# Six pairs of channel tiles in a 4096-to-2048 float32 projection: seven block products of sums for eight block products

## The chip, the cores and the metric

The kernel runs on one core of a Trainium2 chip. The metric is device time in microseconds (us) of that core, as the median of several executions; lower is better. TensorE (PE in the profile) multiplies matrices into PSUM, VectorE (DVE) and ScalarE (ACT) do elementwise work, and the queue of SyncE (SP) issues nearly all DMAs.

## What is computed

One layer for 256 tokens of width 2048, in float32:

```python
h = rmsnorm(x, norm_g); h, gate = adaln(h, c, ada_w, ada_b)
b_gate, c_gate, v, g = split(h @ w_in, 4)        # w_in 2048 x 16384
u = causal_depthwise_conv(c_gate * v, conv_w)    # width 3
y = b_gate * u * silu(g)                         # 256 x 4096
out = rmsnorm(x + gate * (y @ w_out), final_g)   # w_out 4096 x 2048
```

## The kernel before, in words

Every large product is made of three TensorE passes: an operand is split into a rounded part "hi" and a remainder "lo", and hi·hi, hi·lo and lo·hi are summed in PSUM. ACT makes a weight tile's hi part (line 314), DVE its lo part (line 319); the tiles are of 128 partitions by 2048 floats (1 MB). Raw weights, hi parts and lo parts have three buffers each under the tags "raw", "hi" and "lo".

The work has three stages. In the first (bank `mm_s`), part of the input projection runs while the adaLN vectors are formed; a planner with fixed costs sets the order there. In the second (`mm_b`), pairs of channel tiles 8 to 15 are projected, 16 loads of 1 MB at a time in four quarters, and turned into `y`, which is kept in hi and lo parts for all 32 channel tiles (16 pairs). Beside it run 32 pieces that sum the gate vector (lines 546 to 569), one for every second load, at a lower priority. A scheduler places each engine's instructions from priorities and buffers; each engine then runs its own list in order.

The third stage (lines 612 to 707), the output projection, is the one the change rewrites. Four blocks of 512 output columns (`dc`) follow each other. In each, eight loads (`raw_o`, line 666) bring four channel tiles of `w_out` by 512 columns; `out_mm` (lines 621 to 631) runs, for each of the two token tiles of 128 tokens and each channel tile, three matmuls with `y` as the stationary operand and 512 columns as the moving one. That is 24 matmuls of 512 columns for each load, 768 in all. When a block is done, `gated` multiplies by the gate, adds `x`, squares for the norm, and applies `final_g`; in the last block the gate is multiplied into the weights beforehand (line 673) and `x` is put into PSUM as the seed. In this stage raw weights use the "lo" buffers (the first one a "raw" buffer) and the lo parts use the "raw" buffers. `x` and `final_g` are loaded (lines 614 to 616) once the space of the token operand `hT` is free, which is after the last `mm_b` matmul.

Of the kernel before, what the change touches and what calls it, by code (L numbers as in the profile page):

```python
# [8 lines left out]
F32 = mybir.dt.float32  # L9
# [108 lines left out]
def short_conv_layer(ctx: ExitStack, tc: tile.TileContext, x, c, norm_g, ada_w, ada_b, w_in, conv_w, w_out, final_g, out):  # L118
# [9 lines left out]
    adap = ctx.enter_context(tc.tile_pool(name="adap", bufs=2))  # L128
    wpool = ctx.enter_context(tc.tile_pool(name="wpool", bufs=2))
# [8 lines left out]

    def raw_tile(name):
        return wpool.tile([P, SLOT], F32, tag="raw", name=name, bufs=3)  # L140
# [43 lines left out]
    rows1 = const.tile([80, P], F32, tag="rows1", name="rows1")  # L184
    rows2 = const.tile([96, P], F32, tag="rows2", name="rows2")
# [18 lines left out]
    for n, (j, kk) in enumerate(((0, 4), (4, 4), (8, 4), (12, 2), (14, 1), (15, 1))):  # L204
        at = wpool.tile([P, SLOT], F32, tag=("lo", "hi")[n % 2], name="at0", bufs=3)[:, : kk * 2 * NK0 * P]
        at = at.rearrange("p (k s f) -> p k s f", k=kk, s=2)
        if n == 0:
            wpool.tile([P, 32], F32, tag="line3", name="line3", bufs=1)
        for s in range(2):
            nc.sync.dma_start(at[:, :, s, :], adas[:, j : j + kk, s, 0 : NK0 * P])  # L210
        first_ada.extend(at[:, i] for i in range(kk))
# [6 lines left out]
    ones = const.tile([P, P], F32, tag="ones", name="ones")  # L218
# [53 lines left out]
    hT = hpool.tile([P, KT, 2 * T], F32R, tag="big", name="hT")  # L272
    hh_ = hT[:, :, 0:T]
    hl_ = hT[:, :, T : 2 * T]
# [18 lines left out]
    def modulate(k0, nk, sums):  # L293

        ks = slice(k0, k0 + nk)
        sums = sums.rearrange("p (s k) -> p s k", s=2)
        nc.vector.tensor_tensor(out=mod[:, :, ks], in0=sums, in1=bias[:, :, ks], op=ALU.add)
        for k in range(k0, k0 + nk):
            hf = xs[k // CT][:, k % CT, :]
            nc.scalar.activation(hh_[:, k], hf, AF.Identity, bias=mod[:, 0, k : k + 1], scale=mod[:, 1, k : k + 1])  # L300
# [3 lines left out]
            nc.vector.tensor_tensor(out=hl_[:, k], in0=hf, in1=hh_[:, k].bitcast(F32), op=ALU.subtract)  # L304

    def hi_tile():
        return wpool.tile([P, SLOT], F32R, tag="hi", name="hi", bufs=3)

    def lo_tile(lo_tag="lo"):
        return wpool.tile([P, SLOT], F32R, tag=lo_tag, name="lo", bufs=3)  # L310
# [129 lines left out]
    def product(dst, hi, lo, k, i, begins, left, ends):  # L440

        w, h = ((hi, hh_), (hi, hl_), (lo, hh_))[i]

        mm = last_mm[0] = nc.tensor.matmul(dst, w, h[:, k], start=begins and left, stop=ends, skip_group_check=True)  # L444
# [69 lines left out]
    for kind, *step in plan():  # L514
        if kind == "ada":
            ada_piece(*step)
        else:
            ch, k1 = step[0], step[3]
            part(*step)
            if step[2] == 0 and len(acc) in LATER:  # L520
                with tc.issue_after(last_mm[0].ins), behind(ended):
                    if len(acc) == LATER[0]:
                        nc.sync.dma_start(rows2[:, :], conv_w.rearrange("w (k p) -> (w k) p", p=P))
# [31 lines left out]
    def gate_sums(dc, j, at3):  # L555
        nc.sync.dma_start(at3, adas[:, j : j + 2, 2, dc * 512 : (dc + 1) * 512])
        if j == 0:
            gacc[0] = adap.tile([P, 512], F32, tag="gv", name="gacc")
        ga = gacc[0]
        for i in range(2):  # L560
            s = silu_c[:, j + i : j + i + 1]
            if j + i == 0:
                nc.vector.tensor_scalar_mul(ga, at3[:, i, :], s)
            else:
                nc.vector.scalar_tensor_tensor(out=ga, in0=at3[:, i, :], scalar=s, in1=ga, op0=ALU.mult, op1=ALU.add)
        if j + 2 == KT:
            ps = psum.tile([P, 512], F32, tag="sm", name="ps_gate", bufs=2)
            nc.tensor.matmul(ps, ones, ga, start=True, stop=True)  # L568
            nc.vector.tensor_tensor(out=gate(dc), in0=ps, in1=gate(dc), op=ALU.add)

    KP = 8
    n_piece = 0
    for ct in range(NS, NCT, 2):
        for q in QUARTERS:
            bank = psum.tile([P, CT, T], F32, tag="mm", name="mm_b")[:, 0:2]
            col = q * E + ct * P
            for kp in range(0, KT, KP):
# [12 lines left out]
                n_piece += 1  # L590
                if n_piece % 2 == 0:
                    gate_piece()
# [12 lines left out]
            else:  # L605
                nc.vector.tensor_tensor(out=u, in0=bank, in1=u, op=ALU.mult)
                split_y(ys[ct // 2], u)
    while gate_todo:
        gate_piece()


    big = hpool.tile([P, 4, D], F32, tag="big", name="big")
    fg = big[:, 2, :]
    for t in range(TT):
        nc.sync.dma_start(big[:, t, :], x[t * P : (t + 1) * P, :])
    nc.sync.dma_start(fg, final_g.rearrange("(o d) -> o d", o=1).partition_broadcast(P))
    fsq = const.tile([P, TT, 4], F32, tag="fsq", name="fsq")
    EP = 4
    LATE = 3

    def out_mm(po, t, ep, hi, lo):
        for i in range(EP):
            ct = ep * EP + i
            y = ys[ct // 2][:, ct % 2]
            yh = y[:, 0, t * P : (t + 1) * P]
            yl = y[:, 1, t * P : (t + 1) * P]
            o = slice(i * 512, (i + 1) * 512)
            opens = ct == 0 and dc < 3
            nc.tensor.matmul(po, yh, hi[:, o], start=opens, stop=False, skip_group_check=True)  # L629
            nc.tensor.matmul(po, yh, lo[:, o], start=False, stop=False, skip_group_check=True)  # L630
            nc.tensor.matmul(po, yl, hi[:, o], start=False, stop=ct == NCT - 1, skip_group_check=True)  # L631

    part_sum = const.tile([P, TT], F32, tag="part_sum", name="part_sum")

    def finish(t):

        fs = const.tile([P, 1], F32, tag="fs", name="fs", bufs=2)
        nc.scalar.activation(fs, fsq[:, t, 3:4], AF.Sqrt, bias=part_sum[:, t : t + 1])
        nc.vector.reciprocal(fs, fs)
        for c0, n, vector in ((0, 512, True), (512, 512, False), (1536, 512, True), (1024, 512, False)):  # L640
            dd = slice(c0, c0 + n)
            r = big[:, t, dd]
# [8 lines left out]
    for dc in range(4):  # L651
        dcs = slice(dc * 512, (dc + 1) * 512)

        both = [psum.tile([P, TT, 512], F32, tag="mm", name="mm_o") for _ in range(1 + (dc == 3))]
        po = [both[-t][:, t] for t in range(TT)]
        n_ep = NCT // EP
        late = []
        if dc == 3:

            for t in range(TT):  # L660
                nc.scalar.copy(po[t], big[:, t, dcs])
        for ep in range(n_ep):

            first = dc == 0 and ep == 0
            raw = wpool.tile([P, SLOT], F32, tag="raw" if first else "lo", name="raw_o", bufs=3)
            nc.sync.dma_start(
                raw.rearrange("p (k f) -> p k f", k=EP),
                w_out[0, ep * EP * P : (ep + 1) * EP * P, dcs].rearrange("(k p) f -> p k f", p=P),
            )
            if dc == 3:  # L670
# [3 lines left out]
                    out=raw3, in0=raw3, in1=gate(dc).unsqueeze(1).to_broadcast([P, EP, 512]), op=ALU.mult  # L674
                )
            hi, lo = split(raw, SLOT, "raw")
            out_mm(po[0], 0, ep, hi, lo)
            if dc == 3 and ep >= n_ep - LATE:
                late.append((ep, hi, lo))
            else:  # L680
                out_mm(po[1], 1, ep, hi, lo)

        def gated(t, bank, c0, n):

            cs = slice(dc * 512 + c0, dc * 512 + c0 + n)
            r = big[:, t, cs]
            p0 = (dc % 2) * 1024 + t * 512 + c0
            pr = big[:, 3, p0 : p0 + n]
            if dc == 3:
                nc.scalar.activation(pr, bank, AF.Square, scale=D**-0.5, accum_out=fsq[:, t, dc : dc + 1])  # L690
                return
            nc.vector.tensor_tensor(out=pr, in0=bank, in1=gate(dc)[:, c0 : c0 + n], op=ALU.mult)
            nc.vector.tensor_tensor(out=r, in0=r, in1=pr, op=ALU.add)
            nc.scalar.activation(pr, r, AF.Square, scale=D**-0.5, accum_out=fsq[:, t, dc : dc + 1])
            nc.vector.tensor_tensor(out=r, in0=r, in1=fg[:, cs], op=ALU.mult)
            if dc == 2:
                ps = part_sum[:, t : t + 1]
                nc.vector.reduce_sum(ps, fsq[:, t, 0:3], axis=mybir.AxisListType.X)
                nc.vector.tensor_scalar_add(ps, ps, EPS)

        gated(0, po[0], 0, 512)
        if dc == 3:
            finish(0)
        for ep, hi, lo in late:
            out_mm(po[1], 1, ep, hi, lo)
        gated(1, po[1], 0, 512)
    finish(1)


# [22 lines left out]
```

## Time and profile before

| | us |
|---|---|
| median of 3 executions (lowest, highest) | 913.67 (913.61, 914.41) |
| span of the profiled execution, first to last instruction | 911.9 |
| PE busy in it | 895.7 |
| DVE, ACT busy in it | 616.2, 464.6 |
| first matmul of the third stage, last one's start | 729.3, 904.5 |

The profile gives no time of its own execution beside the span; the median of the timings lies 1.8 us above the span, which is what lies around it. Busy times are sums of instruction durations; PE's matmuls are pipelined, so that two of them overlap in the records (a matmul of 512 columns is recorded as 0.39 us, and one starts every 0.23 us). "Idle before, releaser" names what ended an engine's idle time.

### The profile page before, as it was taken

To read this page: it belongs to the slowest core of one execution; us is meant where nothing else is said; L and a number is where in the kernel's file an instruction comes from. 1 tells how busy PE (TensorE), PEld (TensorE's weight loads), DVE (VectorE), ACT (ScalarE), POOL (GpSimd) and SP (SyncE) were. 2 spreads that over 40 slices of the span, in tenths; PEclk is the share of its full clock that TensorE was granted. 3 is DMA by queue.
4 is the path that set the end of the run, shared out by engine and by line. 5 is a ranking of instruction groups with operands and counts; after the bars stand their busy time and mean duration, and the time that the engine had idled before them with its cause. 6 is when DMAs were issued, how large, how long until landed. Compare 5 with 4: busy or idle time off the path is not lost.

```text
span 911.9 us, 16239 instructions
## 1 busy us (share of the span) xinstructions
PE 895.7 (98%) x7047; PEld 858.5 (94%) x7047; DVE 616.2 (68%) x593; ACT 464.6 (51%) x413; POOL 0.7 (0%) x6
## 2 busy tenths in 40 slices
PE   6999999999999999999999999999999999999996
PEld 4999999999999999999999999999999988888885
DVE  4889999989888899765545555545554544555882
ACT  6768856665558756743334433444333333443333
POOL 0000000000000000000000000000000000000000
PEclk9999999999999999999999999999999999999998
DMA  9999999999998698676656665566656486655542
GB/s 309 367 371 353 365 325 351 356 369 352 338 328 275 197 359 301 201 246 197 186 188 197 200 201 186 187 195 200 200 188 188 140 331 231 203 201 186 185 139 92
DMA packets 163752, 227.65 MB, mean 250 GB/s; under 512 B 5680, under 2 KB 104160, under 8 KB 163296
## 3 DMA queue, kind: packets, MB, share of 16 engines
q1 hardware_dynamic: 163552, 226.56, 74.8%
q8 instruction: 55, 0.90, 0.4%
q14 instruction: 17, 0.14, 0.0%
q10 hardware_dynamic: 128, 0.04, 0.0%
HBM read 224.49 MB, written 2.10 MB: 248 GB/s over the span
## 4 chain that ended last, share of the span: by engine, by line
PE 94%; DMA 3%; ACT 1%; SPq 1%; DVE 0%; issue 0%; ACTq 0%
PE mm_b L444 38%; PE mm_s L444 36%; PE mm_o L631 6%; PE mm_o L629 6%; PE mm_o L630 6%; DMA raw_s<-in_sc_w_in_dram 2%; DMA at<-in_ada_w_dram 1%; SPq L210 1%; DMA x<-in_x_dram 1%; ACT hi L314 0%; PE ps_gate L568 0%; PE tp_g L434 0%; ACT acc L465 0%; DVE lo L319 0%; ACT hT L300 0%; SPq L413 0%
## 5 line engine op out<-in xcount | busy, mean ns | idle before, releaser
L444 PE MATMUL mm_s<-hT,hi 128*128 128x256 f32 x2048 | 350.5, 277 | 0.2
L444 PE MATMUL mm_b<-hT,hi 128*128 128x256 f32 x2048 | 348.8, 276 | 0.0
L444 PEld LDWEIGHTS mm_s<-hT,hi 128*128 128x128 f32 x2048 | 308.7, 188 | 1.1 <-ACT hT L300 0.4
L444 PEld LDWEIGHTS mm_b<-hT,hi 128*128 128x128 f32 x2048 | 308.7, 188 | 0.2 <-issue 0.2
L444 PE MATMUL mm_b<-hT,lo 128*128 128x256 f32 x1024 | 282.6, 276 | 0.0
L444 PE MATMUL mm_s<-hT,lo 128*128 128x256 f32 x1024 | 282.2, 277 | 0.2 <-DVE lo L319 0.2
L319 DVE TENSOR_TENSOR lo<-raw,hi 128x2048 fp32r<-128x2048 f32 (+1 forms) x66 | 148.0, 2244 | 136.8 <-ACT hi L314 136.8
L314 ACT CAST hi<-raw 128x2048 fp32r<-128x2048 f32 (+1 forms) x66 | 123.7, 1874 | 200.2 <-PE mm_b L444 156.1
L444 PEld LDWEIGHTS mm_b<-hT,lo 128*128 128x128 f32 x1024 | 192.2, 188 | 0.2 <-issue 0.2
L444 PEld LDWEIGHTS mm_s<-hT,lo 128*128 128x128 f32 x1024 | 191.7, 188 | 0.7 <-DVE lo L319 0.6
L319 DVE TENSOR_TENSOR lo<-raw_s,hi 128x2048 fp32r<-128x2048 f32 (+1 forms) x80 | 147.6, 1850 | 25.6 <-ACT hi L314 24.6
L314 ACT CAST hi<-raw_s 128x2048 fp32r<-128x2048 f32 (+1 forms) x80 | 124.2, 1559 | 72.0 <-PE mm_s L444 59.2
L319 DVE TENSOR_TENSOR lo<-raw_o,hi 128x2048 fp32r<-128x2048 f32 x32 | 73.3, 2292 | 66.3 <-ACT hi L314 66.1
L314 ACT CAST hi<-raw_o 128x2048 fp32r<-128x2048 f32 x32 | 61.0, 1907 | 107.2 <-PE mm_o L631 83.7
L630 PE MATMUL mm_o<-lo,y 128*128 128x512 f32 x256 | 99.7, 391 | 0.0
L629 PE MATMUL mm_o<-hi,y 128*128 128x512 f32 x256 | 99.3, 389 | 0.0
L631 PE MATMUL mm_o<-hi,y 128*128 128x512 f32 x256 | 99.3, 389 | 0.0
L427 DVE SCALAR_TENSOR_TENSOR gv<-at,silu_c,gv 128x512 f32<-128x512 f32 x105 | 78.6, 749 | 2.2 <-DMA at<-in_ada_w_dram 0.3
L465 ACT COPY acc<-mm_s 128x1024 f32<-128x1024 f32 x54 | 54.5, 1012 | 35.9 <-PE mm_s L444 35.9
L630 PEld LDWEIGHTS mm_o<-lo,y 128*128 128x128 f32 x256 | 48.1, 188 | 10.2 <-issue 0.2
L631 PEld LDWEIGHTS mm_o<-hi,y 128*128 128x128 f32 x256 | 48.0, 188 | 10.2 <-issue 0.2
L629 PEld LDWEIGHTS mm_o<-hi,y 128*128 128x128 f32 x256 | 48.1, 188 | 9.9
(89 smaller groups left out, 349.6 us busy)
## 6 DMA issues: line engine op xcount, KB each, us to landing
raw<-in_sc_w_in_dram SPq DMA_DIRECT2D x64, 1024.0 KB, 5.7
raw_s<-in_sc_w_in_dram SPq DMA_DIRECT2D x47, 1024.0 KB, 7.9
raw_o<-in_sc_w_out_dram SPq DMA_DIRECT2D x32, 1024.0 KB, 5.1
at<-in_ada_w_dram SPq DMA_DIRECT2D x114, 256.0 KB, 8.0
raw_s<-in_sc_w_in_dram SPq DMA_DIRECT2D x33, 512.0 KB, 7.1
at_g<-in_ada_w_dram SPq DMA_DIRECT2D x32, 512.0 KB, 7.8
at<-in_ada_w_dram SPq DMA_DIRECT2D x6, 512.0 KB, 9.6
x<-in_x_dram SPq DMA_DIRECT2D x4, 512.0 KB, 6.4
```

The source lines that it names most:

```text
L210: nc.sync.dma_start(at[:, :, s, :], adas[:, j : j + kk, s, 0 : NK0 * P])
L314: nc.scalar.copy(hi[:, :n], raw[:, :n])
L319: nc.vector.tensor_tensor(out=lo[:, :n], in0=raw[:, :n], in1=hi[:, :n].bitcast(F32), op=ALU.subtract)
L427: nc.vector.scalar_tensor_tensor(out=gv, in0=at4[:, i], scalar=c_k, in1=gv, op0=ALU.mult, op1=ALU.add)
L444: mm = last_mm[0] = nc.tensor.matmul(dst, w, h[:, k], start=begins and left, stop=ends, skip_group_check=True)
L465: nc.scalar.copy(acc[ch, q], bank)
L629: nc.tensor.matmul(po, yh, hi[:, o], start=opens, stop=False, skip_group_check=True)
L630: nc.tensor.matmul(po, yh, lo[:, o], start=False, stop=False, skip_group_check=True)
L631: nc.tensor.matmul(po, yl, hi[:, o], start=False, stop=ct == NCT - 1, skip_group_check=True)
```

## The change

For the first 1024 output columns the loads become "two channel tiles by 1024 columns", one for each pair of channel tiles, in the order 0, 1, 10, 2, 11, 3, 12, 4, 13, 5, 14, 6, 15, 7, 8, 9. For the pairs 0 to 9 the 24 matmuls per load stay. For the pairs 10 to 15 the 2×2×2 blocks (two token tiles, two channel tiles, two blocks of 512 columns) are multiplied by Winograd's form of Strassen's scheme: seven products of sums of blocks, 21 matmuls. Sums of the weight blocks are made by DVE for every such load and split like raw weights; sums of the `y` blocks (`forms`) are made in the second stage when such a pair is done, and lie in the buffers of the gate pieces, which therefore are issued for every load instead of every second one. `gather` recombines the products that the four output blocks share. The other 1024 columns run as before.

```diff
+    def token_forms(pair, u):
+        sums = zs[0][:, 0].rearrange("p a (b f) -> p (a b) f", f=P)
...
+        nc.vector.scalar_tensor_tensor(out=s1n, in0=a21, scalar=-1.0, in1=a22, op0=ALU.mult, op1=ALU.subtract)
+        nc.vector.scalar_tensor_tensor(out=s2, in0=s1n, scalar=-1.0, in1=a11, op0=ALU.mult, op1=ALU.subtract)
+        nc.vector.tensor_tensor(out=s3, in0=a11, in1=a21, op=ALU.subtract)
+        nc.vector.tensor_tensor(out=s4, in0=a12, in1=s2, op=ALU.subtract)
...
+        nc.scalar.copy(hi, sums)
+        nc.vector.tensor_tensor(out=lo, in0=sums, in1=hi.bitcast(F32), op=ALU.subtract)
...
-                n_piece += 1
-                if n_piece % 2 == 0:
-                    gate_piece()
+                gate_piece()
...
+    p75 = psum.tile([P, 2, W], F32, tag="mm", name="mm_7")
+    wide = [psum.tile([P, 2, W], F32, tag="mm", name="mm_w") for _ in range(TT)]
+    p1, p6 = (psum.tile([P, W], F32, tag="sm", name="mm_1", bufs=2) for _ in range(2))
...
+    def seven(j, raw):
...
+        sums = w_tile("lo", "sums_o")
+        hi, lo = hi_tile(), lo_tile("raw")
...
+        nc.vector.tensor_tensor(out=s[:, 0:2], in0=b[:, 1:3], in1=b[:, 0:1].to_broadcast([P, 2, W]), op=ALU.subtract)
+        nc.scalar.copy(bh[:, 1:4], b[:, 1:4])
+        nc.vector.tensor_tensor(out=s[:, 2], in0=b[:, 2], in1=s[:, 0], op=ALU.add)
+        nc.vector.tensor_tensor(out=s[:, 3], in0=b[:, 3], in1=s[:, 2], op=ALU.subtract)
+        nc.vector.tensor_tensor(out=bl[:, 1:4], in0=b[:, 1:4], in1=bh[:, 1:4].bitcast(F32), op=ALU.subtract)
+        sh, sl = (v.rearrange("p (b f) -> p b f", f=W) for v in split(sums, SLOT, "raw"))
...
+        triple(p1, y_parts(2 * j, 0), bh[:, 1], bl[:, 1], opens, last)
+        triple(wide[0][:, 1], y_parts(2 * j + 1, 0), bh[:, 3], bl[:, 3])
+        triple(wide[0][:, 0], f(3), bh[:, 2], bl[:, 2])
+        triple(p75[:, 0], f(2), sh[:, 1], sl[:, 1], opens, last)
+        triple(p75[:, 1], f(0), sh[:, 0], sl[:, 0], opens, last)
+        triple(p6, f(1), sh[:, 2], sl[:, 2], opens, last)
+        triple(wide[1][:, 1], y_parts(2 * j + 1, 1), sh[:, 3], sl[:, 3])
...
+    order = (0, 1, 10, 2, 11, 3, 12, 4, 13, 5, 14, 6, 15, 7, 8, 9)
+    for n, j in enumerate(order):
+        raw = w_tile("lo" if n else "raw", "raw_o")
+        load_o(raw, 2 * j, 2, 0, 2 * W)
...
```

`triple` is the three matmuls hi·hi, hi·lo, lo·hi. Smaller parts: small tiles move in SBUF, the token operand is split into 14 and 2 blocks, and the gated ends of the first 1024 columns take 1024 columns at once, after the loop.

On DVE, at the third stage's start, this stood before (`lo<-raw_o` is a weight tile's lo part, `z<-mm_b` the last bank of the second stage taken out):

```order
L319 TENSOR_TENSOR lo<-raw_o,hi 128x2048
L606 TENSOR_TENSOR z_4463<-mm_b,z_4463 128x512
L319 TENSOR_TENSOR lo<-raw_o,hi 128x2048
L397 TENSOR_TENSOR y_4459<-z_4463,y_4459 128x2x256
L319 TENSOR_TENSOR lo<-raw_o,hi 128x2048 x3
```

On DVE after the change, from the lo part of load 2's plain pair (pair 2) on, through pairs 11 and 12 (`sums_o` holds the sums of weight blocks, `lo<-sums_o` is their lo part, `lo<-raw_o` of 1536 that of three of the blocks themselves):

```order
L346 TENSOR_TENSOR lo<-raw_o,hi 128x2048
L720 TENSOR_TENSOR sums_o<-raw_o 128x1024
L722 TENSOR_TENSOR sums_o<-raw_o,sums_o 128x512
L724 TENSOR_TENSOR lo<-raw_o,hi 128x1536
L723 TENSOR_TENSOR sums_o<-raw_o,sums_o 128x512
L346 TENSOR_TENSOR lo<-sums_o,hi 128x2048
L346 TENSOR_TENSOR lo<-raw_o,hi 128x2048
L720 TENSOR_TENSOR sums_o<-raw_o 128x1024
L724 TENSOR_TENSOR lo<-raw_o,hi 128x1536
L722 TENSOR_TENSOR sums_o<-raw_o,sums_o 128x512
L723 TENSOR_TENSOR sums_o<-raw_o,sums_o 128x512
L346 TENSOR_TENSOR lo<-sums_o,hi 128x2048
```

One lo part per load has become six instructions for a load of seven products, and the lo part of the plain load between two such loads stands behind the lo part of the sums. On ACT, before, from the same place, the eight casts of a block simply follow each other:

```order
L314 CAST hi<-raw_o 128x2048 x2
L396 CAST y_4459<-z_4463 128x2x256
L314 CAST hi<-raw_o 128x2048 x8
L694 ACTIVATE big,fsq<-big 128x512 x2
L314 CAST hi<-raw_o 128x2048 x7
```

On ACT after the change (`form_h` belongs to the sums of pair 15's `y`):

```order
L341 CAST hi<-raw_o 128x2048
L721 CAST hi<-raw_o 128x1536
L423 CAST y_4471<-z_4475 128x2x256
L341 CAST hi<-sums_o 128x2048
L623 CAST form_h<-z_4474 128x512
L341 CAST hi<-raw_o 128x2048
L721 CAST hi<-raw_o 128x1536
L341 CAST hi<-sums_o 128x2048
L341 CAST hi<-raw_o 128x2048
```

A second cast now waits for DVE's sums. On PE, where pair 11's matmuls stand after the change (`mm_8263` and `mm_8264` are `p1` and `p6`, `mm_8260` is `p75`, `y_3623` belongs to plain pair 3):

```order
L695 MATMUL mm_w<-hi,form 128x512
L695 MATMUL mm_w<-lo,form 128x512
L695 MATMUL mm_w<-hi,form 128x512
L695 MATMUL mm_8260<-hi,form 128x512
L695 MATMUL mm_8264<-hi,form 128x512
L695 MATMUL mm_w<-hi,y_4467 128x512
L695 MATMUL mm_w<-hi,y_3623 128x512
L695 MATMUL mm_8260<-lo,form 128x512
L695 MATMUL mm_8260<-hi,form 128x512 x2
```

The first matmul that reads the lo part of the sums is the fourteenth from the pair's start (six stand ahead of these rows), and one matmul of the next plain pair has come ahead of it. On SP, before and after around the third stage's first loads:

```order
L666 DMA raw_o<-in_sc_w_out_dram 128x4x512 x4
L615 DMA big<-in_x_dram 128x2048 x2
L616 DMA big<-in_final_g_dram 128x2048
L666 DMA raw_o<-in_sc_w_out_dram 128x4x512 x28
```

```order
L684 DMA raw_o<-in_sc_w_out_dram 128x2x1024 x4
L675 DMA big<-in_x_dram 128x2048 x2
L677 DMA big<-in_final_g_dram 128x2048
L684 DMA raw_o<-in_sc_w_out_dram 128x2x1024 x12
L684 DMA raw_o<-in_sc_w_out_dram 128x4x512 x16
```

The loads' number, size and order stay; `x` and `final_g` stand behind the fourth load in both, and the load of pair 11 is the first one behind them.

More of the change, by code (lines that the diff above doesn't have):

```diff
@@ L442, in product @@
         w, h = ((hi, hh_), (hi, hl_), (lo, hh_))[i]
-        mm = last_mm[0] = nc.tensor.matmul(dst, w, h[:, k], start=begins and left, stop=ends, skip_group_check=True)
+        mm = last_mm[0] = nc.tensor.matmul(dst, w, h[k], start=begins and left, stop=ends, skip_group_check=True)
         if begins and left:
@@ L607, in short_conv_layer @@
                 split_y(ys[ct // 2], u)
+                if ct // 2 in SEVEN:
+                    token_forms(ct // 2, u)
     while gate_todo:
         gate_piece()
[L612 to L618 removed]
@@ L619, in short_conv_layer @@
[L619 to L631, printed above, removed]
@@ new lines, in short_conv_layer, with load_o, y_parts, triple @@
+    fsq = const.tile([P, TT, 3], F32, tag="fsq", name="fsq")
+    part_sum = const.tile([P, TT], F32, tag="part_sum", name="part_sum")
+    LATE = 3
+    def load_o(raw, e0, ne, c0, n):
+        nc.sync.dma_start(
+            raw.rearrange("p (k f) -> p k f", k=ne),
+            w_out[0, e0 * P : (e0 + ne) * P, c0 : c0 + n].rearrange("(k p) f -> p k f", p=P),
+        )
+    def y_parts(ct, t):
+        return [ys[ct // 2][:, ct % 2, h, t * P : (t + 1) * P] for h in range(2)]
+    def triple(dst, y, hi, lo, opens=False, ends=False):
+        for i, (a, b) in enumerate(((0, hi), (0, lo), (1, hi))):
+            nc.tensor.matmul(dst, y[a], b, start=opens and i == 0, stop=ends and i == 2, skip_group_check=True)
@@ new lines, in gather @@
+    def gather():
+        add = lambda out, a, b: nc.vector.tensor_tensor(out=out, in0=a, in1=b, op=ALU.add)
+        nc.scalar.copy(ends[0][:, 1], p1)
+        add(u2, p6, ends[0][:, 1])
+        add(ends[1][:, 1], p75[:, 0], u2)
+        add(ends[0][:, 0], p75[:, 1], u2)
+        add(ends[1][:, 0], p75[:, 1], ends[1][:, 1])
+    order = (0, 1, 10, 2, 11, 3, 12, 4, 13, 5, 14, 6, 15, 7, 8, 9)
+    for n, j in enumerate(order):
+        raw = w_tile("lo" if n else "raw", "raw_o")
+        load_o(raw, 2 * j, 2, 0, 2 * W)
+        load_ends(n - 4)
+        if j in SEVEN:
+            seven(j, raw)
+            if j == SEVEN[-1]:
+                gather()
+            continue
+        hi, lo = split(raw, SLOT, "raw")
+        for t in range(TT):
+            for k in range(2):
+                for d in range(2):
+                    o = slice((k * 2 + d) * W, (k * 2 + d + 1) * W)
+                    triple(
+                        wide[t][:, d], y_parts(2 * j + k, t), hi[:, o], lo[:, o],
+                        n == 0 and k == 0, j == order[-1] and k == 1,
+                    )
@@ L660, in short_conv_layer, with out_mm @@
             for t in range(TT):
-                nc.scalar.copy(po[t], big[:, t, dcs])
-        for ep in range(n_ep):
[L664 to L669, printed above, removed]
+                nc.scalar.copy(po[t], xr[:, t, dcs])
+        def out_mm(t, ep, hi, lo):
+            for i in range(EP):
+                ct = ep * EP + i
+                o = slice(i * W, (i + 1) * W)
+                triple(po[t], y_parts(ct, t), hi[:, o], lo[:, o], ct == 0 and dc < 3, ct == NCT - 1)
+        for ep in range(n_ep):
+            raw = w_tile("lo", "raw_o")
+            load_o(raw, ep * EP, EP, dc * W, W)
             if dc == 3:
```

143 lines of the change are left out of this document (97 added, 46 removed).

## The prediction

> **What bounds the kernel now.** I read the busy shares first, then the slices of the span, then the chain that ended last.
>
> ```profile
> span 911.9 us, 16239 instructions
> PE 895.7 (98%) x7047; PEld 858.5 (94%) x7047; DVE 616.2 (68%) x593; ACT 464.6 (51%) x413; POOL 0.7 (0%) x6
> PEclk9999999999999999999999999999999999999998
> PE mm_b L444 38%; PE mm_s L444 36%; PE mm_o L631 6%; PE mm_o L629 6%; PE mm_o L630 6%; DMA raw_s<-in_sc_w_in_dram 2%; DMA at<-in_ada_w_dram 1%; SPq L210 1%; DMA x<-in_x_dram 1%; ACT hi L314 0%; PE ps_gate L568 0%; PE tp_g L434 0%; ACT acc L465 0%; DVE lo L319 0%; ACT hT L300 0%; SPq L413 0%
> ```
>
> PE is busy throughout at the full clock, and the chain runs through its matmuls from the first stage to the last, the third stage's three lines with 6% each. So I look at that stage alone, in the table of stretches and in the groups of instructions.
>
> ```profile
> 760.00:800.00 40.00, 40.00 (x178) 33.14 (x177) 21.52 (x14) 14.69 (x11) 0.00 (x0) 1.00 0.57 185
> L630 PE MATMUL mm_o<-lo,y 128*128 128x512 f32 x256 | 99.7, 391 | 0.0
> L314 ACT CAST hi<-raw_o 128x2048 fp32r<-128x2048 f32 x32 | 61.0, 1907 | 107.2 <-PE mm_o L631 83.7 <-PE mm_b L444 10.1 <-DMA raw_o<-in_sc_w_out_dram 9.4
> L319 DVE TENSOR_TENSOR lo<-raw_o,hi 128x2048 fp32r<-128x2048 f32 x32 | 73.3, 2292 | 66.3 <-ACT hi L314 66.1
> ```
>
> In 40 us PE has no idle time, while DVE works 21.5 and ACT 14.7. The matmuls have no idle time before them; ACT's casts wait for PE to free a buffer, and DVE's subtractions wait for ACT. So PE sets the pace, and a matmul taken away is worth its spacing, as long as the others keep up. The spacing comes from the timeline of ACT, whose casts keep PE's step of one load:
>
> ```profile
> 757.63 1.91 ACT L314 CAST hi<-raw_o 128x2048 fp32r<-128x2048 f32 x1 [4.43 <-PE mm_o L631]
> 763.07 1.91 ACT L314 CAST hi<-raw_o 128x2048 fp32r<-128x2048 f32 x1 [3.53 <-PE mm_o L631]
> 768.51 1.91 ACT L314 CAST hi<-raw_o 128x2048 fp32r<-128x2048 f32 x1 [3.53 <-PE mm_o L631]
> ```
>
> A load of 24 matmuls takes 5.44 us, so one matmul 0.2267.
>
> **Removed.** Six loads of 24 matmuls become 21: 18 × 0.2267 = **4.08 us** of PE. A load of seven products takes PE 4.76 us, and such a load with a plain one 10.20.
>
> Here the Trainium skill speaks against the change: "TensorE: Matmul & The Clock Gate", section "Back-to-back issue gap", gives about 131 ns for each 512-column matmul in a sustained stream. By that the 18 are worth 2.4 us. The rows above say 0.2267, and the measurement decides.
>
> **Added in the second stage.** For each of six pairs DVE makes four sums of 128x128 (each at most 0.48, the row for 255 columns below), a lo part of 512 columns (0.69), and ACT a cast of 512 (0.61): some 2.6 us on DVE. The gate pieces (two instructions of 0.75) that move behind pair 10 are eight, 12 us of DVE.
>
> ```profile
> 500.00:600.00 100.00, 100.00 (x885) 100.00 (x884) 51.00 (x37) 41.57 (x31) 0.00 (x0) 1.00 0.62 195
> L388 DVE SCALAR_TENSOR_TENSOR z<-z,cw,z 128x255 f32<-128x255 f32 x16 | 7.0, 478 | 0.0
> L396 ACT CAST y<-z 128x512 fp32r<-128x512 f32 x8 | 4.9, 614 | 0.0
> L565 DVE SCALAR_TENSOR_TENSOR gacc<-at_g,silu_c,gacc 128x512 f32<-128x512 f32 x60 | 44.9, 749 | 1.0
> ```
>
> DVE is idle for 49 us of 100 there; even pair 11, some 44 us with all eight pieces and its sums, has 21 us to give for 15. I cost this at nothing; without that cover it would be these 15 us once. The lower ends (`gather`, the adds of 1024 columns) stand in the stretch after the loop, where DVE has 18 us of 40 to spare: nothing too. Nor do I give the moved tiles a cost.
>
> **Added in the third stage.** For a load of seven products DVE has, instead of one lo part (2.292), sums of 1024, 512 and 512 columns and lo parts of 1536 and 2048. Their prices are in rows of other shapes:
>
> ```profile
> L319 DVE TENSOR_TENSOR lo<-raw_s,hi 128x1024 fp32r<-128x1024 f32 x33 | 40.0, 1222 | 5.6 <-ACT hi L314 5.3
> L693 DVE TENSOR_TENSOR big<-big 128x512 f32<-128x512 f32 x6 | 3.9, 684 | 0.0
> 720.51 2.29 DVE L319 TENSOR_TENSOR lo<-raw_o,hi 128x2048 fp32r<-128x2048 f32 x1 [3.15 <-ACT hi L314]
> 722.72 0.68 DVE L604 TENSOR_TENSOR z<-z 128x512 f32<-128x512 f32 x1
> 65.01 2.33 DVE L427 SCALAR_TENSOR_TENSOR gv<-at,silu_c,gv 128x512 f32<-128x512 f32 x3
> 729.40 1.91 ACT L314 CAST hi<-raw_o 128x2048 fp32r<-128x2048 f32 x1 [3.53 <-PE mm_b L444]
> 731.34 2.29 DVE L319 TENSOR_TENSOR lo<-raw_o,hi 128x2048 fp32r<-128x2048 f32 x1 [1.13 <-ACT hi L314]
> ```
>
> 1536 columns lie halfway between 1.222 and 2.292: 1.757. An instruction that waits for nothing starts 0.08 before the recorded end of the one ahead (720.51 + 2.29 = 722.80, next at 722.72); three that each read the one before take 2.33, so 0.04 lies between them; and from ACT's end to DVE's start pass 0.03.
>
> Busy time alone would fit (6.64 + 2.29 = 8.9 of 10.20), but the order on DVE closes a ring with ACT. From the end of one load's last sum to the end of the next one's: cast of the sums 1.91, lo part of the sums 2.21, lo part of the plain load behind it 2.21, sums of 1024 1.14, lo part of 1536 1.68, sum of 512 that the next one reads 0.69 + 0.04, last sum 0.68, two handovers 0.06: **10.62 us** against PE's 10.20. DVE stands idle for 1.9 of these, waiting for the cast, because its next instruction is the lo part of the sums. PE loses 0.42 for each pair of loads, once the lead is used up.
>
> The lead, with 0 at PE's first matmul of the stage: pairs 0 and 1 end at 10.88. The cast for plain pair 2 needs the buffer that pair 1 frees then; a matmul's record (0.39) reaches 0.16 past the next start, so ACT casts from 11.07 to 12.98 and DVE makes the lo part until 15.30. Behind it: sums 1.22 (to 16.44), sum 0.68 + 0.04 (to 17.16), lo part 1.76 (to 18.84), last sum (to 19.44), cast 1.91, lo part 2.29 and handovers, to **23.70**. PE wants that lo part at its fourteenth matmul of pair 11: 3 × 5.44 + 4.76 + 13 × 0.2267 = **24.03**. So pair 11 has 0.33 to spare; pairs 12 to 15 come 4 × 0.42 = 1.68 later relative to PE, which leaves a wait of **1.35 us** in all, in pieces under 0.5 each. Behind pair 15 the plain loads need 2.3 of DVE and 1.9 of ACT in 5.44, and the loss isn't won back, as PE is the bound again.
>
> The bounds of that wait: nothing, if handovers and reads of fresh results cost less than I put; without any overlap of 0.08 the ring takes 10.94 and pair 11 is ready at about 23.95, so 4 × 0.74 - 0.08 = 2.9. I take 1.35, since each of its parts is a row.
>
> **Loads.** `w_out` in rows of 1024 columns isn't in the trace; the nearest rows are the same 1 MB in rows of 512:
>
> ```profile
> raw_o<-in_sc_w_out_dram SPq DMA_DIRECT2D x32, 1024.0 KB, 5.1
> DMA to landing us min/median/max: 5.0/5.1/14.6
> big<-in_final_g_dram SPq DMA_DIRECT2D x1, 1024.0 KB, 11.6
> 729.51 0.82 SPq L615 DMA_DIRECT2D big<-in_x_dram  x2
> 730.98 8.66 SPq L666 DMA_DIRECT2D raw_o<-in_sc_w_out_dram  x3
> 729.32 0.39 PE L629 MATMUL mm_o<-hi,y 128*128 128x512 f32 x1
> 745.64 1.91 ACT L314 CAST hi<-raw_o 128x2048 fp32r<-128x2048 f32 x1 [8.72 <-DMA raw_o<-in_sc_w_out_dram]
> ```
>
> In the ring a load of seven products is issued at the last sum, which frees its buffer, and its data are wanted 1.91 + 2.21 + 2.21 = 6.3 later: 5.1 fits with 1.2 to spare. The exception is pair 11's load: SP issues it at about 6.3 (pair 10's last sum), behind `x` and `final_g`. Before, the load behind these, issued at 730.98, landed at 745.64, 16.3 after the stage's first matmul (729.32), with the same loads ahead of it. `x` waited for the second stage's last matmul; its place now covers 14 of 16 token blocks, and the last two blocks' six matmuls (0.113 each, 885 in the 100 us above) stand behind these, so it goes 0.7 earlier: 15.6. DVE wants it at 15.2 (behind the plain lo part), so pair 11 is **0.4** late. The bounds: landed in time, 0; at 16.3 as before, 1.1. A landing 5.1 after its issue, as if nothing lay ahead, is no nearer row, since 3 MB do.
>
> **Sum.** On the profiled execution 911.9 - 4.08 + 1.35 + 0.4 = 909.6 of span; the median of the timings lies 1.8 above the span, so **911.3** for it.
>
> **The rivals.**
> First, the full gain: the ring turns no slower than PE, because the costs in it are smaller by 0.42 in all, and the load is in time. For it: before, PE's matmuls of this stage have 0.0 idle time. Against: each part of the ring is a measured row. Time: 909.6.
> Second, the ring eats most of the gain: no overlap, and every handover twice as long (ring 11.04, a loss of 0.84 for each pair, pair 11 ready 0.1 past its time). With the late load that is 4 × 0.84 + 0.1 + 0.4 = 3.9, so 913.5, within 0.2%. For it: the ring's steps all lie in series, so each small cost counts four times. Against: the overlaps in the rows.
> Third, and slower: pair 11's load comes late. If it takes from its own issue at 6.3 the same 14.6 as the load behind `x` and `final_g` took, it lands at 20.9 instead of by 15.2, and everything behind it on DVE moves by 5.7: 1.35 + 5.7 - 4.08 = 3.0 slower, 916.7. It decides from a landing 2.7 past 15.2, at 17.9, where the gain is gone; slower by over 0.2% (1.8 us) from 19.7. For it: ACT's single wait of 8.7 for that DMA before, the longest landing in the row. Against: the load now starts 5 us later than those ahead of it, and these go on meanwhile.
> Under this third one, "TensorE: Matmul & The Clock Gate", section "The HAM clock gate", would add to the loss: an idle window of some 3.4 us halves PE's clock for a while. No wait inside the stages shows that here.
> That the change doesn't do what it says is out: the built program has 18 matmuls fewer.
>
> **How the numbers follow.** 0.2% is 1.8 us, about what a measurement of this kernel can tell from no change, so faster is below 911.8. The forecast (waits of 0.7 to 2.2 in all, 910.3 to 911.8) has 0.47, the full gain 0.17, the second rival with all waits above 2.2 up to 913.6 has 0.25, the third 0.11. Faster takes the first two (0.64), within 0.2% the second rival (0.25), slower the third (0.11). The range goes from 909.5 (no wait) to 913.5 (the second rival), and leaves out the third and an edge.
>
> **What would show it.** A third stage on PE that is shorter by 2.3; a gate's sum, which moves from it to the second stage, shortens it by 0.9 more and is no gain:
>
> ```profile
> 751.48 0.86 PE ps_gate L568 x2
> ```
>
> Further: PE waiting in the loads of pairs 12 to 15 for `lo<-sums_o` or the casts, under 0.5 each, with casts of the sums 10.6 apart; a step of 10.2 means the full gain, of 11 the second rival. Pair 11's first cast should start at 14 to 16 after the stage's first matmul; far later is the third. Any wait in the second stage, or behind pair 15, would make the prediction wrong.

## The result, and the profile after

| | before | after |
|---|---|---|
| median, us (11 executions each) | 913.86 | 911.92 |
| lowest, highest | 913.58, 914.55 | 911.56, 912.68 |
| ratio, 95% interval | | 0.9979 [0.9971, 0.9988] |
| span of the profiled execution | 911.9 | 910.2 |

The change is 0.21% faster, 1.9 us. The page of the changed kernel, its busy line and its chain:

```profile
span 910.2 us, 16272 instructions
PE 894.2 (98%) x7029; PEld 854.7 (94%) x7029; DVE 653.5 (72%) x647; ACT 476.1 (52%) x422; POOL 0.7 (0%) x6
PE mm_b L471 38%; PE mm_s L471 38%; PE mm_o L695 10%; PE mm_w L695 7%; PE mm L695 2%; PE tp_idle L258 1%; DMA rows<-in_ada_b_dram 1%; PE sum L380 1%; PE ps_gate L596 0%; PE tp_g L461 0%; PE tp_x L310 0%; ACT hi L341 0%; ACT acc L492 0%; ACT hT L327 0%; ACT mm_s L504 0%; ACT big L787 0%
```

PE has 18 matmuls fewer, DVE 37 us more, and PE is still the chain from end to end. A busy share of 98% hides small waits, since a matmul that starts late is drawn beside the end of the one ahead. They show in the table of stretches (columns: stretch, its length, then busy time and count for PE, PEld, DVE, ACT, POOL, then clock and DMA):

```profile
500.00:600.00 100.00, 100.00 (x873) 99.04 (x872) 65.17 (x63) 40.58 (x31) 0.00 (x0) 1.00 0.74 232
760.00:800.00 40.00, 39.97 (x170) 31.10 (x169) 31.04 (x22) 21.53 (x13) 0.00 (x0) 1.00 0.64 205
```

In the second stage the moved gate pieces and the sums of `y` raise DVE from 51 to 65 us in 100, and PE stays full. In the third, DVE goes from 21.5 to 31.0 in 40, ACT from 14.7 to 21.5, and PE issues 170 matmuls where it issued 178: eight fewer in 40 us are some 1.8 us of waiting, in the stretch of pairs 12 to 15. The waits of PE's weight loads (us in total, times, longest) say for whom:

```profile
PEld mm L695 <- DVE lo L346: 1.4, 4, 0.3
PEld mm L695 <- ACT hi L721: 1.1, 4, 0.3
PEld mm_w L695 <- ACT hi L341: 0.2, 1, 0.2
```

Each is small, and the first two come four times, once for each of these pairs. The casts at line 721 wait themselves, for weights that land: pair 12's, at 755.39, stood 1.44 for its DMA. SP issued that load at 750.19, when pair 11's last sum (749.44) had freed the buffer, so it comes as late as the ring of DVE and ACT comes round. A weight load runs ahead of its matmul, so PE itself loses less than the sum of these waits (2.7; the stage lost 1.9, as follows). How long the stage is on PE, from its first matmul to the start of its last:

```profile
730.63 0.39 PE L695 MATMUL mm_w<-hi,y 128*128 128x512 f32 x1
...
902.35 0.39 PE L695 MATMUL mm_o<-hi,y 128*128 128x512 f32 x1
```

That is 171.72 us. Before it was 729.32 to 904.09, 174.77, with 0.86 for the gate's sum that now lies in the second stage: 173.91. So the change took 2.19 out of the stage, of the 4.08 that 18 matmuls are worth.

One turn of the ring on DVE, from the changed kernel's timeline:

```profile
752.18 2.29 DVE L346 TENSOR_TENSOR lo<-sums_o,hi 128x2048 fp32r<-128x2048 f32 x1 [2.05 <-ACT hi L341]
754.38 2.29 DVE L346 TENSOR_TENSOR lo<-raw_o,hi 128x2048 fp32r<-128x2048 f32 x1
756.59 1.22 DVE L720 TENSOR_TENSOR sums_o<-raw_o 128x1024 f32<-128x1024 f32 x1
757.72 1.75 DVE L724 TENSOR_TENSOR lo<-raw_o,hi 128x1536 fp32r<-128x1536 f32 x1
759.39 0.69 DVE L722 TENSOR_TENSOR sums_o<-raw_o,sums_o 128x512 f32<-128x512 f32 x1
760.11 0.69 DVE L723 TENSOR_TENSOR sums_o<-raw_o,sums_o 128x512 f32<-128x512 f32 x1
762.85 2.29 DVE L346 TENSOR_TENSOR lo<-sums_o,hi 128x2048 fp32r<-128x2048 f32 x1 [2.05 <-ACT hi L341]
```

It takes 10.67 us (752.18 to 762.85). A load of seven products gives DVE five instructions, three sums and two lo parts; the six named with the change are those of such a load with a plain one. The five between the two lo parts of the sums run without a hole, and the only idle time is the 2.05 in which ACT casts what the last sum has just written. ACT has one such cast for each pair of loads:

```profile
744.53 1.48 ACT L721 CAST hi<-raw_o 128x1536 fp32r<-128x1536 f32 x1 [0.86 <-DMA raw_o<-in_sc_w_out_dram]
750.24 1.91 ACT L341 CAST hi<-sums_o 128x2048 fp32r<-128x2048 f32 x1 [4.23 <-DVE sums_o L723]
...
760.91 1.91 ACT L341 CAST hi<-sums_o 128x2048 fp32r<-128x2048 f32 x1 [4.05 <-DVE sums_o L723]
```

The first of these rows is pair 11's load: ACT starts on it at 744.53, 13.9 after the stage's first matmul.

### The profile page after: what moved, and what is told of

Read it like the earlier page. It is cut to its first block, busy times and chain, and to the rows that moved or that the text cites. A ratio compares the mean times of both kernels' runs of the same rounds, so it can differ in the third digit from the quotient of the medians.

```text
span 910.2 us, 16272 instructions
## 1 busy us (share of the span) xinstructions
PE 894.2 (98%) x7029; PEld 854.7 (94%) x7029; DVE 653.5 (72%) x647; ACT 476.1 (52%) x422; POOL 0.7 (0%) x6
## 4 chain that ended last, share of the span: by engine, by line
PE 98%; ACT 1%; DMA 1%; ACTq 0%; issue 0%; DVE 0%
PE mm_b L471 38%; PE mm_s L471 38%; PE mm_o L695 10%; PE mm_w L695 7%; PE mm L695 2%; PE tp_idle L258 1%; DMA rows<-in_ada_b_dram 1%; PE sum L380 1%; PE ps_gate L596 0%; PE tp_g L461 0%; PE tp_x L310 0%; ACT hi L341 0%; ACT acc L492 0%; ACT hT L327 0%; ACT mm_s L504 0%; ACT big L787 0%
## 5 line engine op out<-in xcount | busy, mean ns | idle before, releaser
L341 ACT CAST hi<-raw_o 128x2048 fp32r<-128x2048 f32 x26 | 49.6, 1906 | 60.6 <-PE mm_o L695 36.6
L695 PE MATMUL mm_o<-hi,y 128*128 128x512 f32 x256 | 78.7, 389 | 0.0
L346 DVE TENSOR_TENSOR lo<-raw_o,hi 128x2048 fp32r<-128x2048 f32 x26 | 59.5, 2290 | 24.2 <-ACT hi L341 24.1
L695 PE MATMUL mm_w<-hi,y 128*128 128x512 f32 x184 | 58.2, 390 | 0.0
L695 PEld LDWEIGHTS mm_o<-hi,y 128*128 128x128 f32 x256 | 48.0, 188 | 9.9
L695 PE MATMUL mm_o<-lo,y 128*128 128x512 f32 x128 | 49.5, 389 | 0.0
L593 DVE SCALAR_TENSOR_TENSOR gacc<-at_g,silu_c,gacc 128x512 f32<-128x512 f32 x60 | 45.0, 749 | 5.6 <-DMA at_g<-in_ada_w_dram 4.6
L695 PEld LDWEIGHTS mm_w<-hi,y 128*128 128x128 f32 x184 | 34.5, 188 | 7.7 <-ACT hi L341 0.2
```

What stands on the lines that cost most here:

```text
L341: nc.scalar.copy(hi[:, :n], raw[:, :n])
L346: nc.vector.tensor_tensor(out=lo[:, :n], in0=raw[:, :n], in1=hi[:, :n].bitcast(F32), op=ALU.subtract)
L695: nc.tensor.matmul(dst, y[a], b, start=opens and i == 0, stop=ends and i == 2, skip_group_check=True)
```

## The experiments

**Theory:** the gain is 18 matmuls at 0.2267, less what the ring takes back because it needs 10.67 us where PE needs 10.20. **Rivals:** the waits come from weights that land late ("loads"); a matmul taken away is worth less than its spacing ("price"); other parts of the change cost time ("other parts").

**1. All pairs plain.** `x` and `final_g` are put behind later loads, so that they meet no load that is wanted soon; `load` is the load just issued, and on SP's queue they stay behind it.

```diff
-        load_ends(n - 4)
-        if j in SEVEN:
-            seven(j, raw)
-            if j == SEVEN[-1]:
-                gather()
-            continue
...
+        load_ends(n - 8, load)
```

> All sixteen pairs are plain loads of 24 matmuls here (the sums of the weights, their products and the recombination are left out; the sums of the y blocks are still made in the second stage, unused), and x and final_g are loaded behind the ninth to eleventh load of the stage. Everything else of the change is in it. Theory (the ring of DVE and ACT takes back part of the gain): no wait in the third stage, steps of 5.44 us for each load, 174.1 us for 768 matmuls, so the time of the kernel before: ratio 1.000 to 1.0005 (the upper end if the 0.42 us that the first stage was longer in the profile after belongs to the change). Rival 'the other parts cost' (moved gate pieces, sums of y, moved tiles take back the 2 us): ratio 1.002. Rival 'price' (a matmul taken away is worth 0.131 us, not 0.2267): also 1.000, so this run doesn't tell it.

Measured: 913.65 against 913.47, ratio 1.000 [0.9991, 1.0008]. The stage on PE in its profile:

```profile
729.94 0.39 PE L697 MATMUL mm_w<-hi,y 128*128 128x512 f32 x1
...
903.80 0.39 PE L697 MATMUL mm_o<-hi,y 128*128 128x512 f32 x1
```

173.86, the 173.91 of before. So blocks of 1024 columns, the gate pieces, the sums of `y` and the moved tiles together cost nothing that can be measured (the interval is 0.8 us wide to each side). The recombination (`gather`) isn't in this kernel, but it is in edit 2 below, whose stage is shorter than this one by nearly all that 18 matmuls are worth; "other parts" is out.

**2. One DVE instruction behind another.** The scheduler had put the lo part of 1536 columns (line 724) ahead of the last two sums (for pair 11 ahead of the last one). Here it must follow them:

```diff
-        nc.vector.tensor_tensor(out=s[:, 3], in0=b[:, 3], in1=s[:, 2], op=ALU.subtract)
-        nc.vector.tensor_tensor(out=bl[:, 1:4], in0=b[:, 1:4], in1=bh[:, 1:4].bitcast(F32), op=ALU.subtract)
+        last_sum = nc.vector.tensor_tensor(out=s[:, 3], in0=b[:, 3], in1=s[:, 2], op=ALU.subtract)
+        rest = nc.vector.tensor_tensor(out=bl[:, 1:4], in0=b[:, 1:4], in1=bh[:, 1:4].bitcast(F32), op=ALU.subtract)
+        tc.add_manual_dep(rest.ins, last_sum.ins.name, after, reason="the sums first")
```

> Only the place of one DVE instruction is changed: the lo part of 1536 columns comes behind the last sum, so that DVE makes it while ACT casts the sums. Theory (ring): the ring gets shorter by the 1.68 that then lie beside the cast, 10.67 - 1.68 = 8.99 us for a pair of loads against PE's 10.20, so DVE is idle 0.3 instead of 2.05 before the lo part of the sums, PE's waits in pairs 12 to 15 go (under 0.2 in all), the casts of the sums come 10.2 apart, and the third stage on PE gets 1.7 to 1.9 shorter: 910.0 us, ratio 0.9958 to before (0.9954 to 0.9962). Rival 'loads' (the waits come from weights that land late behind x and final_g): nothing changes, 0.9979. Rival 'price' (18 matmuls at 0.131 us are worth 2.4 us): nothing changes, 0.9979 to 0.9977.

Measured: 909.80 against 913.47, ratio 0.9962 [0.9949, 0.9974]. The ring on DVE now, and the stage on PE:

```profile
761.46 2.29 DVE L346 TENSOR_TENSOR lo<-sums_o,hi 128x2048 fp32r<-128x2048 f32 x1 [0.39 <-ACT hi L341]
764.73 2.29 DVE L346 TENSOR_TENSOR lo<-raw_o,hi 128x2048 fp32r<-128x2048 f32 x1 [0.97 <-ACT hi L341]
766.93 1.22 DVE L720 TENSOR_TENSOR sums_o<-raw_o 128x1024 f32<-128x1024 f32 x1
768.19 0.69 DVE L722 TENSOR_TENSOR sums_o<-raw_o,sums_o 128x512 f32<-128x512 f32 x1
768.91 0.69 DVE L723 TENSOR_TENSOR sums_o<-raw_o,sums_o 128x512 f32<-128x512 f32 x1
769.52 1.75 DVE L724 TENSOR_TENSOR lo<-raw_o,hi 128x1536 fp32r<-128x1536 f32 x1
771.66 2.29 DVE L346 TENSOR_TENSOR lo<-sums_o,hi 128x2048 fp32r<-128x2048 f32 x1 [0.39 <-ACT hi L341]
```

```profile
731.25 0.39 PE L695 MATMUL mm_w<-hi,y 128*128 128x512 f32 x1
...
901.09 0.39 PE L695 MATMUL mm_o<-hi,y 128*128 128x512 f32 x1
```

The lo part covers the cast, and DVE's wait for it falls from 2.05 to 0.39. The turn takes 10.20, PE's own pace: DVE now has a wait of 0.97 for the plain load's cast, which waits for a buffer that PE frees (at 762.79, after 1.36). PE's weight loads have no wait left in the stage, which takes 169.84, 4.02 less than with plain loads alone: 18 matmuls at 0.223. That settles the price, and the same loads at the same places no longer cost PE anything. By its time this kernel is clearly faster than the one before, but its interval overlaps that of the changed kernel (0.9971 to 0.9988); it is the stage's length that tells these two apart.

The same kernel a second time:

> The kernel with the lo part of 1536 columns behind the last sum once more, for a closer interval and a second profile. Theory (ring): ratio 0.9956 to 0.9964, no wait of PE in pairs 12 to 15, third stage on PE 169.8 us. Rival (the first profile was a lucky one): waits of some tenths appear, 0.9970.

Measured: 910.20 against 913.61, ratio 0.9959 [0.9947, 0.9972], again without a wait in the stage, which takes 169.85.

**3. The cast of the sums twice,** alone and together with edit 2, so that the ring gets longer by a known step.

```diff
+        sums_hi = split_hi(sums, SLOT)
+        nc.scalar.copy(sums_hi, sums)
```

> ACT casts the sums of the weights twice, the second time into the same place (no result changes). Theory (ring): the second cast adds 1.83 to the ring, 10.67 + 1.83 = 12.50 us for a pair of loads against PE's 10.20; pair 11's lead of 0.19 turns into a wait of 1.64, and pairs 12 to 15 wait 2.30 each: 10.8 us in all instead of 1.7, so 921 us, ratio 1.0079 (1.007 to 1.009), with casts of the sums 12.5 apart. Rival 'ACT has time to spare' (it is busy for half of the span, so one cast more costs nothing or the single wait of the first pair): 0.998 to 1.000.

> Both edits together: the sums are cast twice, and the lo part of 1536 columns stands behind the last sum, so that it lies beside these casts. Theory (ring): 10.67 + 1.83 - 1.68 = 10.82 us for a pair of loads, 0.62 more than PE; the lead of pair 11 is 0.19 + 1.68 - 1.83 = 0.04, so the waits are 2.4 us in all, and the time 2.4 above that with the place of the lo part alone: ratio 0.9988 (0.998 to 1.000). Rival 'only the place counts' (DVE's order did something else than shorten the ring): as with the place alone, 0.9962.

Measured: 921.40 against 913.61, ratio 1.0086 [1.0070, 1.0101], alone; 914.03 and 1.0004 [0.9995, 1.0013] with edit 2. The casts, alone first (`hi<-sums_o` at line 341 is the first cast of the sums, line 726 the second), then with edit 2 (there line 727 is the second):

```profile
749.73 1.91 ACT L341 CAST hi<-sums_o 128x2048 fp32r<-128x2048 f32 x1 [4.08 <-DVE sums_o L723]
751.54 1.89 ACT L341 CAST hi<-raw_o 128x2048 fp32r<-128x2048 f32 x1
753.34 1.89 ACT L726 CAST hi<-sums_o 128x2048 fp32r<-128x2048 f32 x1
...
762.33 1.91 ACT L341 CAST hi<-sums_o 128x2048 fp32r<-128x2048 f32 x1 [5.72 <-DVE sums_o L723]
...
774.93 1.91 ACT L341 CAST hi<-sums_o 128x2048 fp32r<-128x2048 f32 x1 [5.72 <-DVE sums_o L723]
776.87 1.90 ACT L726 CAST hi<-sums_o 128x2048 fp32r<-128x2048 f32 x1
```

```profile
759.95 1.91 ACT L341 CAST hi<-sums_o 128x2048 fp32r<-128x2048 f32 x1 [2.88 <-DVE sums_o L723]
761.89 1.90 ACT L727 CAST hi<-sums_o 128x2048 fp32r<-128x2048 f32 x1
...
771.02 1.91 ACT L341 CAST hi<-sums_o 128x2048 fp32r<-128x2048 f32 x1 [2.75 <-DVE sums_o L723]
```

Alone the turn is 12.60 (12.50 expected), with edit 2 it is 11.07 (10.82 expected). With edit 2 every turn has the expected order, and two of my steps were too small for it. The second cast starts 1.94 after the first (759.95, 761.89), not 1.83; a cast that writes another place starts 1.81 after it (749.73, 751.54), so that writing the same place is the likely reason. And edit 2 takes 1.54 off the ring, not 1.68: in the changed kernel the lo part (1.67) lies between the sum of 1024 and the sum that reads it (756.59, 757.72, 759.39); without it the second starts 1.26 after the first (766.93, 768.19) instead of the lo part's 1.13, since it reads a fresh result. 10.67 + 1.94 - 1.54 = 11.07 is what was measured, and the second ratio lies just above its range for this reason.

Alone, the scheduler chose again, and the edit did only in part what I meant. In one of the four turns (774.93 to 787.54) the second cast stands straight behind the first, and 10.67 + 1.94 = 12.61 is what was measured. In the other three, as at 749.73, ACT casts the plain load between the two casts of the sums, and DVE makes the plain load's lo part ahead of that of the sums: there the cast that the ring gains is the plain load's, and the second cast lies beside DVE's work. That two of these three turns come out at 12.60 as well was not forecast. The last one takes 13.21 (787.54 to 800.75); the cast that ends it waited for PE to free a buffer, behind a stretch in which PE had half its clock (see the end). The four kernels side by side, PE's pace being 10.20:

| kernel | one turn of the ring, us | third stage on PE, us | above 169.84 |
|---|---|---|---|
| edit 2 | at PE's pace | 169.84 | 0 |
| after | 10.67 | 171.72 | 1.88 |
| cast twice, edit 2 | 11.07 | 173.68 | 3.84 |
| cast twice | 12.60 | 181.93 | 12.09 |

Pair 11's lead is 0.19 in the changed kernel (worked out below), and by the same steps -0.21 and -1.75 in the two with a second cast (the last an estimate, as the order there is another). Four further turns cost 4 × 0.47, 4 × 0.87 and 3 × 2.40 + 3.01; less the lead that is 1.69, 3.69 and 11.96. Each falls short of the measured loss by less than 0.2. PE loses what the ring takes longer, turn by turn. That ACT is idle for half of the span doesn't help.

**4. Further plain loads between the seven-product ones,** as the scheduler orders them, and then with the first sum kept behind the plain load's lo part on DVE.

```diff
-    order = (0, 1, 10, 2, 11, 3, 12, 4, 13, 5, 14, 6, 15, 7, 8, 9)
+    order = (0, 1, 10, 2, 3, 11, 4, 5, 12, 6, 13, 7, 14, 8, 15, 9)
...
+        tc.add_manual_dep(first_sum.ins, last_lo[0].ins.name, after, reason="the plain load first")
```

> The same work as in the changed kernel in another order of pairs, 0 1 10 2 3 11 4 5 12 6 13 7 14 8 15 9: two plain loads instead of one between pairs 10 and 11 and between 11 and 12. Theory (ring): each further plain load gives PE 5.44 us of work and the ring only 2.2 to 4, which is lead of 1.4 or more for the 0.47 that each alternation loses, so PE's waits are under 0.3 in all: 910.0 to 910.3 us, ratio 0.9958 to 0.9962. Rival 'loads': pair 11's load starts later as well, so its wait, if there was one, goes too, but the waits of the later pairs stay: 0.9975. Rival 'price': 0.9979.

> The order of pairs of the run with further plain loads between pairs 10, 11 and 12, but the first sum of a load of seven products is kept behind the lo part of the plain load ahead of it on DVE. Theory: in that run the 1.8 us of PE's wait for a lo part came from DVE standing 4.3 us at a first sum whose weights had not landed, with the plain load's lo part queued behind it; with that lo part ahead the wait goes, and what is left of the ring's loss is 0.3 to 0.9 in pairs 13 to 15: ratio 0.9964 to 0.9971. Rival: the wait came from the order of pairs itself (loads of 1024 columns that come too late for a buffer that frees late); then it stays, 0.9976.

Measured: 911.65 against 913.47, 0.9976 [0.9967, 0.9985], and 911.08 against 913.61, 0.9973 [0.9963, 0.9983]. Both lie above their ranges, the second by 0.0002. The rival "loads" had 0.9975 for the first, but not what the rows show: the waits of the later pairs shrank too, and the weights that came late were pair 14's, far behind `x` and `final_g`. In the first, one wait of PE (1.8) takes the place of most of the small ones; DVE there, ACT's cast for the plain load, and PE's weight load:

```profile
779.39 2.29 DVE L346 TENSOR_TENSOR lo<-sums_o,hi 128x2048 fp32r<-128x2048 f32 x1 [0.39 <-ACT hi L341]
786.01 1.23 DVE L720 TENSOR_TENSOR sums_o<-raw_o 128x1024 f32<-128x1024 f32 x1 [4.32 <-DMA raw_o<-in_sc_w_out_dram]
787.15 2.28 DVE L346 TENSOR_TENSOR lo<-raw_o,hi 128x2048 fp32r<-128x2048 f32 x1
```

```profile
782.81 1.90 ACT L341 CAST hi<-raw_o 128x2048 fp32r<-128x2048 f32 x1 [3.45 <-PE mm_w L695]
```

```profile
789.49 0.19 PEld L695 LDWEIGHTS mm_w<-lo,y 128*128 128x128 f32 x1 [1.76 <-DVE lo L346]
```

DVE stands 4.32 us at a sum whose weights have not landed; the lo part that PE waits for is queued behind it, though its cast had ended at 784.71. With that lo part ahead, this wait is gone, as expected, and these are left:

```profile
PEld mm L696 <- DVE lo L346: 0.7, 2, 0.3
PEld mm_o L696 <- ACT hi L341: 0.7, 1, 0.7
PEld mm L696 <- ACT hi L723: 0.4, 2, 0.3
PEld mm_w L696 <- ACT hi L341: 0.2, 1, 0.2
```

The ring's waits shrink against the changed kernel. One of 0.7 stands where the stage's second half begins (`mm_o`). The first kernel of this order has it too, with 0.6; the changed kernel has none there. In both the last load of seven products has one plain load behind it instead of three, which I had not counted; that this is the reason was not tried. The two intervals overlap, so that the times alone do not tell the two kernels apart; the stage's length on PE does, 172.36 in the first and 171.29 with the lo part ahead.

**5. `x` and `final_g` later,** the edit of run 1 in the changed kernel.

> Only x and final_g are issued later, behind the ninth, tenth and eleventh load of the third stage instead of ahead of pair 11's load. Theory (ring): pair 11's data lay ready 1.4 us before DVE took them, so the ring keeps its 10.67 and gains at most some tenths of lead: waits of 1.4 to 1.9 us in pairs 12 to 15, ratio 0.9974 to 0.9979. Rival 'loads': the waits go, 910.0 us, ratio 0.9958.

Measured: 914.12 against 913.47, ratio 1.0008 [0.9999, 1.0017], by the ratios 2.6 us slower than the changed kernel. DVE and PE's waits:

```profile
741.40 1.23 DVE L722 TENSOR_TENSOR sums_o<-raw_o 128x1024 f32<-128x1024 f32 x1 [0.25 <-DMA raw_o<-in_sc_w_out_dram]
...
753.72 1.23 DVE L722 TENSOR_TENSOR sums_o<-raw_o 128x1024 f32<-128x1024 f32 x1 [3.23 <-DMA raw_o<-in_sc_w_out_dram]
754.86 2.28 DVE L346 TENSOR_TENSOR lo<-raw_o,hi 128x2048 fp32r<-128x2048 f32 x1
```

```profile
PEld mm_w L697 <- ACT hi L341: 1.7, 2, 1.4
PEld mm L697 <- DVE lo L346: 0.9, 3, 0.3
PEld mm_w L697 <- DVE lo L346: 0.8, 1, 0.8
PEld mm L697 <- ACT hi L341: 0.5, 1, 0.5
```

Neither theory had this. Moving these loads away from pair 11's did not remove the ring's waits, so "loads" is out as the cause of the 1.88: pair 11's weights were there at 741.40, 5.1 after their issue (736.27) and 11.3 after the stage's start (730.11) instead of 13.9, and nothing came of it. But DVE's order changed again: pair 12's sum stands ahead of a plain load's lo part and waits 3.23 for its weights, though `x` was issued only later, at 760.51. Of PE's waits, 0.8 (at 757.20) are for the lo part behind that sum. The longest, 1.4 at 787.00, comes behind pair 14, whose load was issued at 771.03, between `x` and `final_g`, and landed at 778.42, 7.4 after its issue where the median is 5.1. So both the order and the 3 MB beside the loads have a part; how much of the 2.6 us is the one and how much the other wasn't tried. This profiled execution (912.85) was 1.3 faster than the median, so its rows hold only part of the loss.

## Why the prediction was right, point by point

911.3 was forecast as 2.4 below a median of 913.67; the ratio is 1.9 below, and the stage on PE, forecast 2.3 shorter, is 2.19 shorter. The mechanism was the one forecast, but two of its terms were off, in opposite directions: 1.35 for the ring and 0.4 for pair 11's load make 1.75, where the ring alone took 1.88 and that load nothing. That the sum came so near is luck.

- **4.08 for 18 matmuls:** right. 4.02 between run 1 and run 2. By the 131 ns of the Trainium skill ("TensorE: Matmul & The Clock Gate", section "Back-to-back issue gap") it would have been 2.4; this case's trace does not agree with that figure, here 223 ns. The changed kernel alone could not have told the two apart: its 2.19 is nearer to 2.4 than to 4.08.
- **Second stage and moved tiles at nothing:** right, run 1.
- **The ring, 10.62 and 1.35 of waits:** the mechanism right, the term too small. The turn is 10.67. Pair 11's lo part ends at 752.18 + 2.29 = 754.47, 23.84 after the stage's start where I had 23.70, so its lead is 24.03 - 23.84 = 0.19 where I had 0.33. 4 × 0.47 - 0.19 = 1.69 was to be expected of these; 1.88 was measured, and the 0.2 between them I have not traced.
- **Pair 11's load, 0.4 late:** this step failed. I took its landing from the row before, where the load behind `x` and `final_g` landed 16.3 after the start of the stage, and shifted it to 15.6. ACT began its cast at 13.9, 7.7 after the load's issue where the row before had 14.6, and DVE took the data at 745.91, when it was done with the plain load's lo part, not when they landed. In the old kernel SP issued three weight loads within the 8.66 us from 730.98, now one in that time (at 736.80); that less stood beside it may be why it landed sooner, but this wasn't tried.
- **The third rival** turned on that same load, and decided nothing. In run 5 a load did come late, at another place, in a kernel that lost more than the change gains; the late load's share of that loss is open.
- **What would show it:** waits under 0.5, casts 10.67 apart, none in the second stage and none behind pair 15, as said; the first cast of pair 11 came 0.1 before the window that I gave.

What I did not see is that the ring's loss was a choice of the scheduler: I took DVE's order as given, priced each of its parts, and never asked whether the 1.68 of the lo part could lie beside the cast. The order stood in the built program before any run, and the sum for it (some 9 against 10.20) could have been made from the same rows.

## What to carry to other kernels

When work is taken off the bound engine, add up the ring of the others, instruction by instruction in the order in which they are queued, and compare it with the bound engine's new step: busy shares (DVE 72%, ACT 52%) say nothing of a ring that turns 0.47 too slowly. If an engine idles in the ring while another works on its last result, look for an instruction ahead of that result that could stand behind it; here one such move took 1.88 us off the stage, nearly as much again as the whole change (2.19). And after any edit that lets a scheduler choose again, read the new order before the time: in runs 4 and 5 it put something that waits ahead of something that was wanted, and in run 3 it moved a cast that was meant to stay.

## What was not expected of the hardware

In the kernel with two casts PE's matmuls came 0.43 apart for a while, though PE was waiting for nothing any more. Its table of stretches around pair 14:

```profile
790.00:793.60 3.60, 1.78 (x7) 0.96 (x6) 2.32 (x2) 3.60 (x3) 0.00 (x0) 1.00 0.51 203
793.60:797.00 3.40, 3.40 (x10) 2.59 (x10) 3.40 (x2) 0.82 (x1) 0.00 (x0) 0.52 0.68 190
```

After 3.6 us in which PE issued seven matmuls, the granted clock was 0.52 in a stretch of 3.4 us, and ten matmuls went through where fifteen would have; in finer slices it is 0.50 from 793.8 to 797.2. Waits of the same kind at pairs 11 and 12 left it at 1.00, though PE did no more in the second of these rows than ahead of the drop:

```profile
753.40:756.40 3.00, 1.67 (x7) 1.13 (x7) 2.93 (x2) 3.00 (x3) 0.00 (x0) 1.00 0.25 101
764.50:767.90 3.40, 1.56 (x7) 0.76 (x5) 1.83 (x1) 3.40 (x3) 0.00 (x0) 1.00 0.65 263
```

"TensorE: Matmul & The Clock Gate" of the Trainium skill, section "The HAM clock gate", has a half clock after an idle window of some 3.4 us and the full one again after a busy window of that length; the trace agrees with the half and with its 3.4 us, but PE was not idle for a whole such window, only mostly waiting. What decides that one such stretch drops the clock and another doesn't, no run here shows. In the changed kernel itself, with no wait over 0.3, the clock stayed at 1.00 through the stage.

The profiled executions also differ ahead of all this: `mm_s` begins between 24.9 and 26.9 us after the span's start, and for the kernel of edit 2 at 26.9 once and at 25.1 once, so a single span is no measure of a change of 2 us; the stage's own length is.
